# Neighbourhood attention on one core: two score groups per PSUM bank, and transposes that fill their banks one after another

## The chip, the cores and the metric

The kernel runs on one core of a Trainium2 chip. A core has a matrix engine (PE, with its weight loads shown apart as PEld), a vector engine (DVE), a scalar engine (ACT), a general engine (POOL) and queues that issue DMA transfers (SP is the one used most). PE writes its results to PSUM, a memory of eight banks; one bank holds 512 float32 values on each of 128 partitions. The metric is the device time of one execution in microseconds (us).

## The reference

One layer of a bidirectional encoder with 2048 tokens on a grid of 32 rows by 64 columns, 1024 features, 16 heads of 64. All numbers are float32.

```
h = rmsnorm(x, norm_0)
q, k, v, gate = split(h @ w_in, 4)
for each grid row r:                      # a query sees 8 key rows and 16 key columns
    s = q[r] . k[rows rs..rs+8, 32 columns round the block] / 8
    s = where(column is valid, s + bias, -1e30)
    p = softmax(s);  o[r] = p . v
x = x + (o * silu(gate)) @ w_out
return rmsnorm(x, norm_f)
```

## The kernel before

The kernel has three parts in time. First come the projections (`h @ w_in`), made of 128x512 products in two-part float32r (tile `pp`). Then comes a stretch of about 340 us in which attention and the last projections, later the first output products (`po`), alternate on PE. Last come the remaining output products (`py`).

Attention goes by pairs of heads `p` and blocks `T` of eight grid rows of queries. A block sees a stretch of key rows (`KEY_ROWS`): 11 rows for T=0, 15 for T=1 and T=2, 12 for T=3. Queries are cut into eight column strips `g` of 8x8 = 64 queries; two strips make a group `C` (`GROUPS`), and a group sees 2 or 3 strips of keys (`WIDE`). With R = 8 x key rows, a group's scores are 128 partitions (two strips of 64 queries) by `R * WIDE[C]` columns, for each of the two heads `s`. `order` lists the 32 pairs (p, T): eight with T=0, then sixteen with T=1 and 2, then eight with T=3.

The main loop makes one cycle for each entry `m` of `order`, and a last one. On PE a cycle is, in program order:

- some 12 to 21 matmuls of `pp` or `po`, given out by `feed`;
- `turns(m - 1)`: 44 transposes of the probabilities of the entry before, two at a time (h = 0 on partitions 0 to 63, h = 1 on 64 to 127), into six banks `ph[b, h]` with 8, 8 and 6 tiles of 64 columns for b = 0, 1, 2. A finished bank is copied to the tile `pta`: by ACT for h = 0, by DVE for h = 1 (`copy`);
- `scores(2m)` for the groups C = 0, 1 and `scores(2m + 1)` for C = 2, 3: for each group and each of two heads a bank, and 4 matmuls, each of 64 rows by 64 columns of the array. A float32 matmul runs as two passes, so the trace shows 32 records for 16 instructions. The query strip `h` picks the half of the output partitions, the head `s` the half of the rows that are read;
- `values(m - 1)`: 16 matmuls of `pta` with the values, into one bank `o`.

For each group and head DVE then adds the bias and takes the row's extreme (L1297, the reader of the score bank), and ACT takes the exponential (L1303). `normalise` multiplies by the reciprocal of the sum: for `scores(2m)` on POOL, for `scores(2m + 1)` on POOL (its first group) and on DVE (its second group). That happens in the next cycle at the latest, ahead of that cycle's transposes.

All PSUM tiles come from one pool of eight banks. A tile gets a bank as banks come free, and the first matmul into it waits until the last reader of the bank's tile before it is done. One bank is usually held by the `pp` or `po` product that is under way across the cycle. Instructions stand on each engine in the order in which the program makes them; there is no other scheduler.

Lines of the profile: L1288 score matmuls, L1343 transposes, L1334 and L1332 the copies by ACT and DVE, L1362 value matmuls, L1297 and L1303 the work on the scores, L1315 and L1313 `normalise` on POOL and DVE.

Of the kernel before, what the change touches and what calls it, by code (L numbers as in the profile page):

```python
# [39 lines left out]
WIDE = [2, 3, 3, 3]  # L40
# [25 lines left out]
def linear():  # L66
    at, n = {}, 0
    for strips in [(0,), (1, 2), (3, 4), (5, 6), (7,)]:
        for s in range(2):
            for strip in strips:  # L70
                for g in range(max(strip - 1, 0), min(strip + 2, 8)):
                    at[s, strip, g] = n
                    n += 1
    return at
# [3 lines left out]
def build(ctx, tc, x, xr, xt, wg, bias, w_out, n0, nf, out):  # L78
    nc = tc.nc
# [48 lines left out]
    def bank(n, name):  # L128
        return banks.tile([128, n], F32, name=name, tag="bank")
# [140 lines left out]
    for n, (k, j, ph, c) in enumerate(halves):  # L270
        a = (KINDS[k] + j, ph)
# [948 lines left out]
    order = [(p, 0) for p in range(NP)] + [(p, T) for p in range(NP) for T in (1, 2)] + [(p, 3) for p in range(NP)]  # L1220
# [52 lines left out]

    X, PT, ST = {}, {}, {}

    def scores(i, between=None):
        p, T, cs = pairs[i]
        kt, qt = KT[p, T], QT[p, T]
        r0, r1 = KEY_ROWS[T]
        got = []  # L1280
        R = (r1 - r0) * 8
        for C in cs:
            pst = [bank(R * WIDE[C], f"s{s}") for s in range(2)]
            for h, g in enumerate(GROUPS[C]):
                c0 = 8 * FIRST[g]
                for s in range(2):
                    a = slice(s * 64, s * 64 + 64)
                    nc.tensor.matmul(pst[s][h * 64:h * 64 + 64], qt[a, g * 64:g * 64 + 64],  # L1288
                                     kt[a, :r1 - r0, c0:c0 + 8 * WIDE[C]].rearrange("p r (s c) -> p s r c", c=8),
                                     start=True, stop=True)  # L1290
            got.append((C, pst))
        ST[i] = st = tiny.tile([128, 12], F32, name="st")
        for j, (C, pst) in enumerate(got):
            X[i, C] = [xp([128, 512], F32, f"x{s}")[:, :R * WIDE[C]] for s in range(2)]
            for s in range(2):
                o = 2 * j + s
                nc.vector.tensor_tensor_reduce(X[i, C][s], pst[s], EM[p, ROW_TYPE[T]][C > 0][s], -1.0, 1e38,  # L1297
                                               OP.add, OP.min, st[:, o:o + 1])
            if between and j == 0:
                between()  # L1300
            for s in range(2):
                o = 2 * j + s
                nc.scalar.activation(X[i, C][s], X[i, C][s], AF.Exp, bias=st[:, o:o + 1], scale=-1.0,  # L1303
                                     accum_out=st[:, 4 + o:5 + o])
# [14 lines left out]
    spots = linear()  # L1319

    def turns(m):
        p, T = order[m]
        k = 8 * (KEY_ROWS[T][1] - KEY_ROWS[T][0])
        PT[m] = pt([128, 3072], F32, "pta")
        t = PT[m].rearrange("p (n h c) -> p h n c", h=2, c=64)
        ph = {(b, h): bank((512, 512, 384)[b], f"ph{h}") for b in range(3) for h in range(2)}
        left = {(b, h): (8, 8, 6)[b] for b in range(3) for h in range(2)}

        def copy(b, h):
            o, i_ = t[:k, h, b * 8:b * 8 + (8, 8, 6)[b]], ph[b, h][:k].rearrange("p (n c) -> p n c", c=64)  # L1330
            if h:
                nc.vector.tensor_copy(o, i_)  # L1332
            else:
                nc.scalar.activation(o, i_, AF.Copy)  # L1334

        group = {g: C for C in range(4) for g in GROUPS[C]}
        lists = [sorted((group[g] // 2, n, s, strip, g) for (s, strip, g), n in spots.items() if n % 2 == h) for h in range(2)]
        for two in zip(*lists):
            for h, (late_, n, s, strip, g) in enumerate(two):
                q = slice(64 * h, 64 * h + 64)  # L1340
                b, o = n // 16, n // 2 % 8 * 64
                at = (strip - FIRST[g]) * k
                nc.tensor.transpose(ph[b, h][:k, o:o + 64], X[2 * m + late_, group[g]][s][q, at:at + k], ident[q, q])  # L1343
                left[b, h] -= 1
            for b, h in sorted(left):
                if left[b, h] == 0:
                    left[b, h] = -1
                    copy(b, h)
# [172 lines left out]
    def split_rows():  # L1521
        n = ready["split"]
        if rows_due():
            split_og(n)
            ready["split"] += 1
            return True
# [264 lines left out]
    for m in range(cycles + 1):  # L1791
        a = amount[m] - 8
        begin(m)
        feed(8)
        if m:
# [10 lines left out]
            for k in range(3):  # L1806
                if m == 1 and k == 2:
                    pass
                elif a > 12 or not any(due_here) and (k < 1 or k < 2 and m > 8 and m % 2 == 0):
                    got = split_rows()  # L1810
# [11 lines left out]
        if m:  # L1822
            turns(m - 1)
        if m == cycles:
            all_loads()
            feed(6)
            while next(outs, 0) != 0:
                due(1)
            land_T2()
            for n in range(3):  # L1830
                form_rows(n, 1)
        else:
            scores(2 * m)
            if m == 0:
                feed(first)
            scores(2 * m + 1, lambda: normalise(2 * m))
            if m == 0:
                consume(2, turn=True)
# [42 lines left out]
```

## Time and profile before

| | us |
|---|---|
| median of 3 runs | 1006.15 (1005.45 to 1006.79) |
| the profiled execution | 1005.34 |
| its span | 1003.4 |
| PE busy | 995.4 (99%) |
| PEld busy | 797.1 (79%) |
| DVE busy | 771.9 (77%) |
| ACT busy | 520.4 (52%) |
| POOL busy | 149.5 (15%) |
| granted clock of PE, mean | 0.998 |

A row of the timeline gives the start, the duration, the engine, the line, the operation, the tiles written and read, shapes, and how many instructions were merged into it; behind it in brackets stands the idle time of the engine before it and what ended it. A PE matmul's duration runs to its modelled end, and matmuls overlap, so that a busy PE can still hold back the next matmul: there the idle time of PEld, whose load stands just ahead of the matmul, tells of the wait.

### The profile page before, as it was taken

To read this page: it belongs to the slowest core of one execution; us is meant where nothing else is said; L and a number is where in the kernel's file an instruction comes from. 1 tells how busy PE (TensorE), PEld (TensorE's weight loads), DVE (VectorE), ACT (ScalarE), POOL (GpSimd) and SP (SyncE) were. 2 spreads that over 40 slices of the span, in tenths; PEclk is the share of its full clock that TensorE was granted. 3 is DMA by queue.
4 is the path that set the end of the run, shared out by engine and by line. 5 is a ranking of instruction groups with operands and counts; after the bars stand their busy time and mean duration, and the time that the engine had idled before them with its cause. 6 is when DMAs were issued, how large, how long until landed. Compare 5 with 4: busy or idle time off the path is not lost.

```text
span 1003.4 us, 19549 instructions
## 1 busy us (share of the span) xinstructions
PE 995.4 (99%) x6904; PEld 797.1 (79%) x6904; DVE 771.9 (77%) x1704; ACT 520.4 (52%) x1271; POOL 149.5 (15%) x233
## 2 busy tenths in 40 slices
PE   9999999999999999999999999999999999999997
PEld 7888888888888888888888777777777777778886
DVE  6899888997666866676765776778888888887876
ACT  7862344565434523343433465676767657564443
POOL 0000001321100000000000133243332323222010
PEclk9999999999999999999999999999999999999999
DMA  8943547777957755655566787879888688799564
GB/s 300 328 136 89 196 144 250 242 249 265 349 154 224 242 154 172 213 186 183 205 199 201 211 272 233 273 228 291 267 262 273 184 263 275 212 362 355 140 177 115
DMA packets 149833, 227.66 MB, mean 227 GB/s; under 512 B 13608, under 2 KB 65064, under 8 KB 149736
## 3 DMA queue, kind: packets, MB, share of 16 engines
q1 hardware_dynamic: 147144, 222.09, 68.8%
q0 software_dynamic: 2160, 3.93, 2.3%
q8 instruction: 54, 0.88, 0.4%
q10 hardware_dynamic: 432, 0.40, 0.1%
q14 instruction: 43, 0.35, 0.1%
HBM read 160.31 MB, written 66.06 MB: 226 GB/s over the span
## 4 chain that ended last, share of the span: by engine, by line
PE 99%; ACT 1%; DVE 0%; issue 0%
PE pp L448 40%; PE pv L614 13%; PE py L1658 10%; PE o L1362 8%; PE s L1288 7%; PE ph L1343 4%; PE pp L394 2%; PE po L1566 2%; PE pv L729 2%; PE po L1568 2%; PE pp L396 2%; PE pp L392 2%; PE po L1570 2%; ACT x L1303 0%; PE zp L135 0%; PE prb L242 0%
## 5 line engine op out<-in xcount | busy, mean ns | idle before, releaser
L448 PE MATMUL pp<-h,f 128*128 128x512 f32 x576 | 185.4, 389 | 0.0
L1315 POOL TENSOR_SCALAR x<-x,st 128x360 f32<-128x360 f32 (+5 forms) x192 | 106.3, 570 | 528.9 <-DVE st L1308 528.2
L448 PE MATMUL pp<-t,f 128*128 128x512 f32 x702 | 171.3, 389 | 0.0
L448 PEld LDWEIGHTS pp<-t,f 128*128 128x128 f32 x702 | 131.8, 188 | 27.4
L1303 ACT ACTIVATE x<-x,st 128x360 f32<-128x360 f32 (+5 forms) x256 | 134.2, 525 | 26.4 <-DVE st L1297 26.4
L448 PEld LDWEIGHTS pp<-h,f 128*128 128x128 f32 x576 | 108.1, 188 | 22.6
L448 PE MATMUL pp<-l,f 128*128 128x512 f32 x288 | 112.1, 389 | 0.0
L1297 DVE CUSTOM_DVE_ANT_0 x<-s,em 128x360 f32<-128x360 f32 (+5 forms) x256 | 102.5, 454 | 1.8 <-PE s L1288 1.4
L431 DVE TENSOR_TENSOR f<-raw,f 128x512 fp32r<-128x512 f32 x105 | 75.7, 726 | 19.6 <-ACT f L430 19.5
L1362 PEld LDWEIGHTS o<-pta,vt 120*64 120x64 f32 (+2 forms) x1024 | 68.8, 137 | 22.6 <-DVE st L1297 15.2
L1362 PE MATMUL o<-pta,vt 120*64 120x192 f32 (+5 forms) x1024 | 83.4, 316 | 0.3 <-issue 0.3
L430 ACT ACTIVATE f<-raw 128x512 fp32r<-128x512 f32 x105 | 63.5, 622 | 37.5 <-DVE raw L437 22.0
L1332 DVE COPY pta<-ph 120x512 f32<-120x512 f32 (+5 forms) x96 | 56.0, 638 | 33.5 <-PE ph L1343 33.2
L1334 ACT ACTIVATE pta<-ph 120x512 f32<-120x512 f32 (+5 forms) x96 | 46.8, 558 | 62.9 <-PE ph L1343 62.8
L1288 PE MATMUL s<-kt,q 64*64 64x360 f32 (+5 forms) x1024 | 78.6, 420 | 0.2 <-ACT pta L1334 0.2
L448 PEld LDWEIGHTS pp<-l,f 128*128 128x128 f32 x288 | 54.1, 188 | 11.2
L1288 PEld LDWEIGHTS s<-kt,q 64*64 64x64 f32 x1024 | 41.5, 131 | 22.0 <-ACT pta L1334 6.4
L614 PE MATMUL pv<-wh,t 128*128 128x512 f32 x176 | 56.1, 389 | 0.0
L448 PE MATMUL pp<-sixths,f 128*128 128x512 f32 x198 | 52.7, 389 | 0.0
L469 POOL TENSOR_TENSOR tmp<-tmp,rb 128x512 f32<-128x512 f32 x18 | 28.4, 1579 | 158.3 <-DVE tmp L466 140.9
L1343 PEld LDWEIGHTS ph<-ident,x 64*120 64x120 f32 (+2 forms) x1408 | 42.5, 128 | 11.3 <-issue 9.2
L1658 PE MATMUL py<-woh,f 128*128 128x512 f32 x160 | 50.6, 390 | 0.0
(226 smaller groups left out, 1870.6 us busy)
## 6 DMA issues: line engine op xcount, KB each, us to landing
raw<-in_wg_dram SPq DMA_DIRECT2D x124, 256.0 KB, 5.1
row<-in_xr_dram SPq DMA_DIRECT2D x32, 256.0 KB, 5.7
vd<-v SPq DMA_DIRECT2D x32, 256.0 KB, 3.4
sgd<-sg SPq DMA_DIRECT2D x32, 256.0 KB, 5.7
q<-qd SPq DMA_DIRECT2D x32, 256.0 KB, 5.6
sgt<-sgd SPq DMA_DIRECT2D x32, 256.0 KB, 6.6
ogd<-og SPq DMA_DIRECT2D x32, 256.0 KB, 2.9
kt<-kd SPq DMA_DIRECT2D x16, 480.0 KB, 6.8
```

What stands on the lines that cost most here:

```text
L430: nc.scalar.activation(t[:, 0], src, AF.Copy)
L431: nc.vector.tensor_tensor(t[:, 1], src, t[:, 0].bitcast(F32), OP.subtract)
L448: nc.tensor.matmul(B[n, P], t[:, int(m == 2), c], x[k][int(m == 1)], start=P in (1, 6, 5) and k == 0 and m == 0, stop=k == 3 and m == 2, s ...
L614: nc.tensor.matmul(p, a[:, o], b, start=P in (1, 6, 5) and k == 0 and m == 0, stop=k == 3 and m == 2, skip_group_check=True)
L1288: nc.tensor.matmul(pst[s][h * 64:h * 64 + 64], qt[a, g * 64:g * 64 + 64], kt[a, :r1 - r0, c0:c0 + 8 * WIDE[C]].rearrange("p r (s c) -> p s ...
L1297: nc.vector.tensor_tensor_reduce(X[i, C][s], pst[s], EM[p, ROW_TYPE[T]][C > 0][s], -1.0, 1e38, OP.add, OP.min, st[:, o:o + 1])
L1303: nc.scalar.activation(X[i, C][s], X[i, C][s], AF.Exp, bias=st[:, o:o + 1], scale=-1.0, accum_out=st[:, 4 + o:5 + o])
L1315: nc.gpsimd.tensor_scalar(X[i, C][s], X[i, C][s], st[:, o:o + 1], 1.0, op0=OP.mult, op1=OP.mult)
L1332: nc.vector.tensor_copy(o, i_)
L1343: nc.tensor.transpose(ph[b, h][:k, o:o + 64], X[2 * m + late_, group[g]][s][q, at:at + k], ident[q, q])
L1362: nc.tensor.matmul(o[s * 64:s * 64 + 64, g0 * 64:g1 * 64], vt[:k, strip, s * 64:s * 64 + 64], t[:k, n * 64:(n + g1 - g0) * 64], start=stri ...
L1658: nc.tensor.matmul(B[m, P], t[:, a, c], b, start=P in (1, 6, 5) and k == 0 and i == 0, stop=k == 3 and i == 2, skip_group_check=True)
```

## The change

Two things are changed, both on PE.

The scores. Where five strips of keys fit a bank (5R <= 512, that is 11 or 12 key rows: T=0 and T=3) the groups C = 0 (2R columns) and C = 1 (3R columns) of one head share one bank, so that `scores(2m)` takes two banks in place of four. In all entries the four matmuls of a group come in another order: both query strips of head 0, then both of head 1. Before, the heads alternated.

The transposes. The six banks hold 6, 8 and 8 tiles for b = 0, 1, 2, and the list is sorted by bank first, so that a bank is filled before the next is begun. Before, the list was sorted by group first: all tiles of C = 0, 1 came ahead of those of C = 2, 3, whatever their bank.

```diff
+    def score_places(cs, R):
+        at = {"order": [(C, s) for C in cs for s in range(2)]}
+        if cs[0] == 0 and 5 * R <= 512:
+            for s in range(2):
+                b = bank(5 * R, f"s{s}")
+                at[0, s], at[1, s] = b[:, :2 * R], b[:, 2 * R:]
+        else:
+            for C, s in at["order"]:
+                at[C, s] = bank(R * WIDE[C], f"s{s}")
+        return at
     def scores(i, between=None):
...
-        for C in cs:
-            pst = [bank(R * WIDE[C], f"s{s}") for s in range(2)]
+        places = score_places(cs, R)
+        for C, s in places["order"]:
             for h, g in enumerate(GROUPS[C]):
                 c0 = 8 * FIRST[g]
-                for s in range(2):
-                    a = slice(s * 64, s * 64 + 64)
-                    nc.tensor.matmul(pst[s][h * 64:h * 64 + 64], qt[a, g * 64:g * 64 + 64],
...
+                a = slice(s * 64, s * 64 + 64)
+                nc.tensor.matmul(places[C, s][h * 64:h * 64 + 64], qt[a, g * 64:g * 64 + 64],
...
     def turns(m):
-        ph = {(b, h): bank((512, 512, 384)[b], f"ph{h}") for b in range(3) for h in range(2)}
-        left = {(b, h): (8, 8, 6)[b] for b in range(3) for h in range(2)}
+        ends = (6, 14, 22)
+        size = (6, 8, 8)
+        ph = {(b, h): bank(size[b] * 64, f"ph{h}") for b in range(3) for h in range(2)}
+        left = {(b, h): size[b] for b in range(3) for h in range(2)}
...
-        lists = [sorted((group[g] // 2, n, s, strip, g) for (s, strip, g), n in spots.items() if n % 2 == h) for h in range(2)]
+        home = lambda n: sum(n // 2 >= e for e in ends)
+        lists = [sorted((home(n), group[g] // 2, n, s, strip, g) for (s, strip, g), n in spots.items() if n % 2 == h) for h in range(2)]
...
-                b, o = n // 16, n // 2 % 8 * 64
+                o = (n // 2 - ends[b] + size[b]) * 64
```

No engine gets more or fewer instructions by this. Two places show what moves, both on PE in a cycle that does the transposes and values of an entry with T=0 and the scores of the next one; rows of equal tiles that follow each other are merged with a count behind.

The scores of the groups C = 0 (176 columns) and C = 1 (264 columns), before: `s0` is the bank of head 0, `s1` that of head 1.

```order
L1288 MATMUL s0_5785<-kt_5545,q_5528 64x176
L1288 MATMUL s1_5786<-kt_5545,q_5528 64x176
L1288 MATMUL s0_5785<-kt_5545,q_5528 64x176
L1288 MATMUL s1_5786<-kt_5545,q_5528 64x176
L1288 MATMUL s0_5791<-kt_5545,q_5528 64x264
L1288 MATMUL s1_5792<-kt_5545,q_5528 64x264
L1288 MATMUL s0_5791<-kt_5545,q_5528 64x264
L1288 MATMUL s1_5792<-kt_5545,q_5528 64x264
```

The same place, and the first of C = 2 behind it, now:

```order
L1297 MATMUL s0_5779<-kt_5541,q_5524 64x176 x2
L1297 MATMUL s1_5780<-kt_5541,q_5524 64x176 x2
L1297 MATMUL s0_5779<-kt_5541,q_5524 64x264 x2
L1297 MATMUL s1_5780<-kt_5541,q_5524 64x264 x2
L1297 MATMUL s0_5802<-kt_5541,q_5524 64x264 x2
L1297 MATMUL s1_5803<-kt_5541,q_5524 64x264 x2
```

Four bank tiles (5785, 5786, 5791, 5792) have become two (5779, 5780), and the two matmuls on the same half of the rows now stand next to each other.

The transposes, before, from the last tile of the first ACT bank (`ph0_5729`) to the last of the first DVE bank (`ph1_5730`); the tiles `x0_5651` and `x1_5652` belong to C = 2:

```order
L1343 MATMUL ph0_5729<-ident_163,x1_5633 88x64
L1343 MATMUL ph1_5734<-ident_163,x1_5627 88x64
L1343 MATMUL ph0_5731<-ident_163,x0_5632 88x64
L1343 MATMUL ph1_5734<-ident_163,x0_5626 88x64
L1343 MATMUL ph0_5731<-ident_163,x1_5633 88x64
L1343 MATMUL ph1_5734<-ident_163,x1_5627 88x64
L1343 MATMUL ph0_5731<-ident_163,x0_5651 88x64
L1343 MATMUL ph1_5730<-ident_163,x0_5651 88x64
L1343 MATMUL ph0_5731<-ident_163,x0_5651 88x64
L1343 MATMUL ph1_5730<-ident_163,x1_5652 88x64
```

Now, the last tiles of the first two banks (`ph0_5723`, `ph1_5724`) and what follows; `x0_5645` belongs to C = 2:

```order
L1355 MATMUL ph1_5724<-ident_163,x0_5626 88x64
L1355 MATMUL ph0_5723<-ident_163,x0_5626 88x64
L1355 MATMUL ph1_5724<-ident_163,x1_5627 88x64
L1355 MATMUL ph0_5723<-ident_163,x1_5621 88x64
L1355 MATMUL ph1_5724<-ident_163,x0_5645 88x64
L1355 MATMUL ph0_5725<-ident_163,x1_5627 88x64
L1355 MATMUL ph1_5726<-ident_163,x1_5627 88x64
```

Of the 22 pairs of transposes the first ACT bank was full with the 8th and the first DVE bank with the 12th; now both are full with the 6th. The first transpose that needs a tile of C = 2 was in the 11th pair; now it is in the 6th.

More of the change, by code (lines that the diff above doesn't have):

```diff
@@ L1279, in scores @@
         r0, r1 = KEY_ROWS[T]
-        got = []
         R = (r1 - r0) * 8
-        for C in cs:
-            pst = [bank(R * WIDE[C], f"s{s}") for s in range(2)]
+        places = score_places(cs, R)
+        for C, s in places["order"]:
             for h, g in enumerate(GROUPS[C]):
                 c0 = 8 * FIRST[g]
-                for s in range(2):
-                    a = slice(s * 64, s * 64 + 64)
[L1288 to L1291, printed above, removed]
+                a = slice(s * 64, s * 64 + 64)
+                nc.tensor.matmul(places[C, s][h * 64:h * 64 + 64], qt[a, g * 64:g * 64 + 64],
+                                 kt[a, :r1 - r0, c0:c0 + 8 * WIDE[C]].rearrange("p r (s c) -> p s r c", c=8),
+                                 start=True, stop=True, skip_group_check=True)
+        got = [(C, [places[C, s] for s in range(2)]) for C in cs]
         ST[i] = st = tiny.tile([128, 12], F32, name="st")
@@ L1325, in turns @@
         t = PT[m].rearrange("p (n h c) -> p h n c", h=2, c=64)
-        ph = {(b, h): bank((512, 512, 384)[b], f"ph{h}") for b in range(3) for h in range(2)}
-        left = {(b, h): (8, 8, 6)[b] for b in range(3) for h in range(2)}
+        ends = (6, 14, 22)
+        size = (6, 8, 8)
+        ph = {(b, h): bank(size[b] * 64, f"ph{h}") for b in range(3) for h in range(2)}
+        left = {(b, h): size[b] for b in range(3) for h in range(2)}
         def copy(b, h):
-            o, i_ = t[:k, h, b * 8:b * 8 + (8, 8, 6)[b]], ph[b, h][:k].rearrange("p (n c) -> p n c", c=64)
+            o, i_ = t[:k, h, ends[b] - size[b]:ends[b]], ph[b, h][:k].rearrange("p (n c) -> p n c", c=64)
             if h:
@@ L1336, in turns @@
         group = {g: C for C in range(4) for g in GROUPS[C]}
-        lists = [sorted((group[g] // 2, n, s, strip, g) for (s, strip, g), n in spots.items() if n % 2 == h) for h in range(2)]
+        home = lambda n: sum(n // 2 >= e for e in ends)
+        lists = [sorted((home(n), group[g] // 2, n, s, strip, g) for (s, strip, g), n in spots.items() if n % 2 == h) for h in range(2)]
         for two in zip(*lists):
-            for h, (late_, n, s, strip, g) in enumerate(two):
+            for h, (b, late_, n, s, strip, g) in enumerate(two):
                 q = slice(64 * h, 64 * h + 64)
-                b, o = n // 16, n // 2 % 8 * 64
+                o = (n // 2 - ends[b] + size[b]) * 64
                 at = (strip - FIRST[g]) * k
```

## The prediction

> **What bounds the kernel now.** I read the page first: its busy times and the chain that ended last.
>
> ```profile
> span 1003.4 us, 19549 instructions
> ...
> PE 995.4 (99%) x6904; PEld 797.1 (79%) x6904; DVE 771.9 (77%) x1704; ACT 520.4 (52%) x1271; POOL 149.5 (15%) x233
> ...
> PE 99%; ACT 1%; DVE 0%; issue 0%
> ```
>
> PE is on the chain for 99% of the span, so whatever shortens PE's stream shortens the kernel, and what other engines gain or lose counts only where PE waits. A busy PE hides short waits, however, since the modelled end of a matmul reaches over the next one. So I next read the groups by line for the weight loads alone, over the attention cycles (575.45 to 897.5 us): the idle time ahead of a load tells of a matmul that was held back.
>
> ```profile
> L1343 PEld LDWEIGHTS ph<-ident,x 64*120 64x120 f32 (+2 forms) x1364 | 41.2, 128 | 10.9 <-issue 8.8 <-POOL x L1315 2.1
> L1288 PEld LDWEIGHTS s<-kt,q 64*64 64x64 f32 x992 | 40.5, 131 | 21.1 <-ACT pta L1334 6.4 <-DVE pta L1332 3.7 <-issue 2.5
> ```
>
> The score loads wait for the two copies of the transposes (`pta`): the banks that the scores want are still being emptied. The timeline of one cycle (transposes of an entry with 11 key rows, scores of the next) shows how that comes about.
>
> ```profile
> 593.22 1.59 POOL L1315 TENSOR_SCALAR x<-x,st 128x264 f32<-128x264 f32 x2 [0.27 <-DVE st L1308]
> ...
> 595.69 1.43 PE L1343 MATMUL ph<-ident,x 64*88 64x64 f32 x44
> ...
> 596.43 1.46 ACT L1334 ACTIVATE pta<-ph 88x512 f32<-88x512 f32 x3 [3.07 <-PE ph L1343]
> 596.63 1.75 DVE L1332 COPY pta<-ph 88x512 f32<-88x512 f32 x3 [2.08 <-PE ph L1343]
> ...
> 597.05 2.31 PE L1288 MATMUL s<-kt,q 64*64 64x176 f32 x32
> 597.94 0.27 PEld L1288 LDWEIGHTS s<-kt,q 64*64 64x64 f32 x8 [0.18 <-ACT pta L1334]
> 598.30 0.33 DVE L1297 CUSTOM_DVE_ANT_0 x<-s,em 128x176 f32<-128x176 f32 x1
> ...
> 598.43 0.46 PEld L1288 LDWEIGHTS s<-kt,q 64*64 64x64 f32 x8 [0.23 <-DVE pta L1332]
> ...
> 599.29 2.37 PEld L1362 LDWEIGHTS o<-pta,vt 88*64 88x64 f32 x32 [0.40 <-DVE st L1297]
> 599.29 2.61 PE L1362 MATMUL o<-pta,vt 88*64 88x128 f32 x32
> ```
>
> From the first score matmul to the first value matmul pass 2.24 us (597.05 to 599.29). In that time the copies by ACT run until 597.89 and those by DVE until 598.38, and one bank is wanted twice: with one bank held by the projection, seven are left for eight score tiles, so the last one (C = 3, head 1) gets the bank of C = 0, head 0, and waits until DVE has read it. DVE does that only behind its copies, from 598.30 to 598.63; PE goes on at about 598.7.
>
> How long the same work takes without a wait is seen in the first cycle, where nothing has been transposed yet and the two halves of the scores stand alone: 176 + 264 columns in one piece, 264 + 264 in the other.
>
> ```profile
> 561.94 0.97 PE L1288 MATMUL s<-kt,q 64*64 64x176 f32 x16
> ...
> 566.70 1.12 PE L1288 MATMUL s<-kt,q 64*64 64x264 f32 x16
> ...
> 561.94 0.51 PEld L1288 LDWEIGHTS s<-kt,q 64*64 64x64 f32 x16 [0.35 <-issue]
> ```
>
> 88 columns more cost 0.15 us, which is 1.70 ns for each column of a group. The four groups of a cycle have 968 columns with 11 key rows, 1320 with 15, 1056 with 12. Beyond the 440 columns of the first piece that makes 0.97 + 528 x 1.70 ns = 1.87 us, 0.97 + 880 x 1.70 ns = 2.47 us and 0.97 + 616 x 1.70 ns = 2.02 us for a cycle without waits. The view by stretches, for L1288 alone, gives what the cycles take: seven cycles with scores of 11 key rows, sixteen with 15, eight with 12.
>
> ```profile
> 575.45:646.60 71.15, 16.17 (x224) 8.85 (x224) 1.00 0.85 255
> 646.60:814.00 167.40, 40.67 (x512) 21.16 (x512) 1.00 0.82 253
> 814.00:897.50 83.50, 19.66 (x256) 10.45 (x256) 1.00 0.85 274
> ```
>
> So the waits inside the scores are 16.17 - 7 x 1.87 = 3.1 us, 40.67 - 16 x 2.47 = 1.2 us and 19.66 - 8 x 2.02 = 3.5 us, together 7.8 us: 0.44 us in each short cycle and 0.07 us in a long one, where the longer matmuls give the copies time. That is the most that earlier banks can bring in the scores.
>
> **The change part by part.** *Shared banks (short cycles).* The scores then want six banks and seven are to be had. No tile waits for a bank that this cycle's scores have used, so the wait for DVE's read goes. The six are, as the program gives them out, a free one, then those of the transposes, in the order in which they are copied. C = 2 starts 0.75 us after the first score matmul (440 columns at 1.70 ns) and C = 3 at 1.20 us, which is 597.80 and 598.25 in the cycle above. Even with the copies as late as now, C = 2 would find the first DVE copy and the second ACT copy about done, and C = 3 the third ACT copy (597.89).
>
> *The transposes' order.* The two first banks are full with the 6th of 22 pairs in place of the 8th (ACT) and 12th (DVE). A pair takes about 1.43 / 22 = 0.065 us at most, so the first ACT copy starts at least 0.1 us earlier, the first DVE copy about 0.2 to 0.3 us (never before ACT's). The widths change places:
>
> ```profile
> L1334 ACT ACTIVATE pta<-ph 88x512 f32<-88x512 f32 x14 | 7.5, 588 | 14.8 <-PE ph L1343 14.8
> L1334 ACT ACTIVATE pta<-ph 88x384 f32<-88x384 f32 x7 | 3.4, 487 | 0.0
> L1332 DVE COPY pta<-ph 88x512 f32<-88x512 f32 x14 | 9.0, 682 | 13.8 <-PE ph L1343 13.8
> L1332 DVE COPY pta<-ph 88x384 f32<-88x384 f32 x7 | 3.8, 544 | 0.0
> ```
>
> The short copy is now the first of three, so ACT's first copy ends 0.2 us earlier (0.1 from its start, 0.1 from its width) and DVE's first about 0.4 us. The three together take as long as before; DVE's last ends about 0.3 us earlier. ACT's last can only start when the last transposes are done, so it ends hardly earlier. In the long cycles, which still take eight banks, C = 1 wants the first DVE and second ACT copies, C = 2 the second DVE and third ACT copies, and C = 3 DVE's third copy and its read of C = 0. With everything on DVE 0.3 us earlier these come in time: most of the 1.2 us goes.
>
> *Two waits that a late copy keeps.* In one short and one long cycle ACT comes late to its first copy, because it does other work.
>
> ```profile
> 815.43 0.54 PE L1288 MATMUL s<-kt,q 64*64 64x192 f32 x2
> 816.16 2.17 PE L1288 MATMUL s<-kt,q 64*64 64x192 f32 x30 [0.19 <-ACT pta L1334]
> ...
> 815.53 1.45 ACT L1334 ACTIVATE pta<-ph 120x512 f32<-120x512 f32 x3
> ...
> 689.88 1.47 ACT L1334 ACTIVATE pta<-ph 120x512 f32<-120x512 f32 x3 [1.25 <-PE ph L1343]
> ```
>
> The chain of work in order of time (start, us, what) shows the scores of the second:
>
> ```profile
> 688.90 1.44 PE ph L1343 x37
> 690.34 2.72 PE s L1288 x30
> ```
>
> In the first, the scores take 0.54 + 2.17 = 2.71 us in place of 2.02, and only 0.1 us comes back through the narrower first copy: 0.6 us stays. In the second, the first copy starts at 689.88 and will end 0.49 us later, at 690.37, when the scores have just begun; their head 1 waits for it, and the copies behind it are as late: an estimated 0.15 us stays.
>
> *The other order of the four matmuls of a group.* The four use the four quarters of the array, and in the piece at 561.94 all run side by side: 16 loads of 131 ns (the mean of the PEld row above), 2.1 us of loads, lie within 0.51 us. Any order of the four should do the same. The new order puts two that read the same 64 rows next to each other; the value matmuls, which all read the same 88 rows, show that neighbour: 32 loads of at least 0.13 us lie within 2.37 us of PEld, under 2.61 us of matmuls. I cost this at nothing; if the cover failed, it would cost as the rival below says.
>
> The Trainium skill, "TensorE: Matmul & The Clock Gate", Part 3 (packing small matmuls), says that a weight load overlaps matmuls in flight only when it goes to another group of rows. By that rule the new order would lose, and the rows just quoted speak against it.
>
> *The wait that is added.* DVE's first read of a shared bank waits for C = 1 as well, which is done 0.97 us after the scores start (the first piece): at 598.02 in the cycle above, against 598.30 at which DVE gets there now and about 598.05 once its copies end earlier. Behind it on DVE stand the other seven reads, and behind those ACT's exponentials; PE waits for them only at the next transposes. So it costs nothing, and would cost PE nothing if DVE began at 598.30 as today.
>
> *The transposes want C = 2 earlier*, in the 6th pair in place of the 11th, 0.3 us. In the cycle above POOL has normalised by 594.81, 0.88 us before the transposes. The tightest cycles are like this one:
>
> ```profile
> 665.75 1.83 POOL L1315 TENSOR_SCALAR x<-x,st 128x360 f32<-128x360 f32 x2 [1.42 <-DVE st L1308]
> ...
> 667.36 1.51 PE L1343 MATMUL ph<-ident,x 64*120 64x64 f32 x44
> ```
>
> POOL ends at 667.58, 0.22 us after the first transpose; of its two tiles the second, from head 1, is now first used in the 8th pair, 7 x 0.065 = 0.45 us in. 0.2 us is left, and DVE, which feeds POOL, gets earlier too. Short cycles get about 0.4 us shorter while DVE's reads get 0.2 us earlier, so they lose 0.2 us of 0.88. Nothing.
>
> **Sum.** 7.8 - 0.6 - 0.15 = 7.0 us. After the scores come the values; they want DVE's third copy (at most 598.38 + 0.14 us for its width, if it started no earlier) and would start at 597.05 + 1.80 = 598.85, so the wait does not pass on to them. The profiled execution took 1005.34 us, 0.81 us below the median of the runs; 1005.34 - 7.0 = 998.3, and against the median 1006.15 - 7.0 = 999.1 us, which I forecast.
>
> **The rivals.** *Only the shared banks bring something* (0.15): the long cycles keep their 1.2 us, as the third ACT copy and DVE's read come no earlier in effect. Then 5.8 us are gained, 1000.3 us. For it: ACT's last copy ends as now. Against it: the rows give DVE 0.3 us.
>
> *The new neighbours get in each other's way* (0.08, slower). If a load can't run beside a matmul on the same rows, as soon as it stands right behind it, each pass of a group exposes one load: 8 passes in 32 cycles are 256 x 0.131 = 33.5 us, and 33.5 - 7.0 = 26.5 us are lost: 1032.6 us. It decides from 7.0 / 256 = 27 ns for each pass. Against it stand the loads of the values, and that the third load of a group at 561.94 already had a running matmul on its rows.
>
> *The banks don't come free as the change wants* (0.05): the next cycle's products or the values take up the bank that is saved, and PE waits at another place for about the same time. Then the time stays within 0.2%, 1005 us by an estimate. Against it: behind the scores only one tile, `o`, is wanted before the copies are all done.
>
> My forecast has 0.72. The range goes from 997.2 (all 7.8 us and 1.1 us for the scatter of runs and small waits of the transposes) to 1002.5 (half of the sum): it takes in the first rival and leaves out the others. A change of 0.2%, about 2 us, is what can be told from none. So: faster 0.87 (the forecast and the first rival), within 0.2% 0.05 (the third), slower 0.08 (the second).
>
> **What would show it.** In the profile after: the scores' busy time per stretch near 13.2, 39.7 and 16.8 us; next to no idle time of score loads put down to DVE's or ACT's copies; DVE's first copy starting with ACT's; the value and transposes rows as long as now; the score loads as closely packed as at 561.94. Wrong would be: longer spacing of the passes within a group, idle time ahead of the transposes put down to POOL, or the waits found again at the values.

## The result and the profile after

The changed kernel took 998.74 us in the median of six runs (996.9 to 1003.56), the kernel before 1006.0 us beside it (1005.45 to 1009.27, six runs): a ratio of 0.993, 95% interval 0.9906 to 0.9954. Forecast were 999.1 us and 997.2 to 1002.5.

The execution that was profiled is the longest of the six: 1003.56 us, span 1001.5. What the change does in attention shows in it as well as in any other; what it loses behind attention is met in the kernel before as well, as will be seen. First its page, the same lines as before:

```profile
span 1001.5 us, 19560 instructions
...
PE 991.0 (99%) x6904; PEld 793.1 (79%) x6904; DVE 772.4 (77%) x1704; ACT 520.4 (52%) x1271; POOL 149.5 (15%) x233
...
PE 93%; DMA 4%; DVE 2%; ACT 1%; issue 0%; SPq 0%; DVEq 0%
```

DMA has 4% of the chain that ended last, where it had none: a transfer now comes late somewhere. In the scores (now L1297) the waits for copies are gone. The groups by line, weight loads over the attention cycles:

```profile
L1355 PEld LDWEIGHTS ph<-ident,x 64*120 64x120 f32 (+2 forms) x1365 | 41.3, 128 | 11.3 <-issue 9.2 <-POOL x L1324 2.1
L1297 PEld LDWEIGHTS s<-kt,q 64*64 64x64 f32 x992 | 36.3, 132 | 17.8 <-ACT pta L1345 0.4
```

ACT's 6.4 us have become 0.4, DVE's 3.7 are gone, and the transposes wait for POOL as long as before (2.1). The view by stretches, for the scores alone (length of the stretch, then PE busy):

```profile
576.32:644.37 68.05, 13.05 (x224) 7.82 (x224) 1.00 0.90 265
644.37:810.02 165.65, 39.32 (x512) 18.75 (x512) 1.00 0.83 256
810.02:890.71 80.69, 16.82 (x256) 9.70 (x256) 1.00 0.88 280
```

Forecast were 13.2, 39.7 and 16.8. The three sum up to 69.2 us against 76.5, 7.3 us less, and the stretches to 314.4 us against 322.05, 7.7 us less. The timeline of the cycle that the prediction showed, POOL and DMA left out:

```profile
595.67 1.43 PE L1355 MATMUL ph<-ident,x 64*88 64x64 f32 x44
596.27 1.75 DVE L1343 COPY pta<-ph 88x384 f32<-88x384 f32 x3 [1.43 <-PE ph L1355]
596.30 1.46 ACT L1345 ACTIVATE pta<-ph 88x384 f32<-88x384 f32 x3 [2.64 <-PE ph L1355]
...
597.03 1.86 PE L1297 MATMUL s<-kt,q 64*64 64x176 f32 x32
...
598.13 0.34 DVE L1306 CUSTOM_DVE_ANT_0 x<-s,em 128x176 f32<-128x176 f32 x1
...
598.82 1.23 PEld L1374 LDWEIGHTS o<-pta,vt 88*64 88x64 f32 x18 [0.40 <-DVE st L1306]
```

From the first score matmul to the first value matmul pass 1.79 us (597.03 to 598.82), where it was 2.24; the prediction's 1.80 was the cycle without a wait. DVE's copies begin with ACT's.

The last values stand behind transposes with no scores in between, and start 1.36 us after the first transpose in place of 1.74 (897.50 to 899.24 before):

```profile
890.71 1.43 PE L1355 MATMUL ph<-ident,x 64*96 64x64 f32 x44
892.07 2.69 PE L1374 MATMUL o<-pta,vt 96*64 96x128 f32 x32
```

So from the first transpose of attention to the last values it is 315.75 us now (576.32 to 892.07) and was 323.79 (575.45 to 899.24): 8.0 us gained, 1.0 more than forecast. Of these the profiled execution gives 5.3 back behind attention. The timeline of DVE and PE there:

```profile
919.50 0.69 DVE L1682 TENSOR_TENSOR u<-py,xp 128x512 f32<-128x512 f32 x1 [1.43 <-PE py L1670]
931.12 0.69 DVE L1643 TENSOR_TENSOR s<-raw 128x512 f32<-128x512 f32 x1 [10.93 <-DMA raw<-ogd]
...
933.16 0.47 PE L1670 MATMUL py<-woh,f 128*128 128x512 f32 x1 [2.82 <-DVE y L1450]
```

DVE stands at a sum (S1 of the third pair of row tiles, L1643) until the load `raw<-ogd` has landed; behind it in DVE's order stands the `y` that would free a bank for PE, and PE is idle for 2.82 us. Before, PE did not notice the wait for the same load:

```profile
930.96 0.69 DVE L1631 TENSOR_TENSOR s<-raw 128x512 f32<-128x512 f32 x1 [3.68 <-DMA raw<-ogd]
```

The load lands at nearly the same time in both profiles (930.96 and 931.12), but DVE comes to it 7 us earlier now. It is not that the transfers keep their time when attention gets shorter: in the profile of e4 (below), whose attention is as short, the load has landed by 922.65.

```profile
922.65 0.69 DVE L1643 TENSOR_TENSOR s<-raw 128x512 f32<-128x512 f32 x1 [2.00 <-DMA raw<-ogd]
```

The question that the experiments had to settle besides the parts of the change: is this wait its price?

### The profile page after: what moved, and what is told of

Its sections match the earlier page's. It is cut to its first block, busy times and chain, and to the rows that moved or that the text cites. A ratio compares the mean times of both kernels' runs of the same rounds, so it can differ in the third digit from the quotient of the medians.

```text
span 1001.5 us, 19560 instructions
## 1 busy us (share of the span) xinstructions
PE 991.0 (99%) x6904; PEld 793.1 (79%) x6904; DVE 772.4 (77%) x1704; ACT 520.4 (52%) x1271; POOL 149.5 (15%) x233
## 4 chain that ended last, share of the span: by engine, by line
PE 93%; DMA 4%; DVE 2%; ACT 1%; issue 0%; SPq 0%; DVEq 0%
PE pp L448 40%; PE pv L614 13%; PE o L1374 8%; PE s L1297 7%; PE py L1670 5%; PE ph L1355 4%; PE pp L394 2%; PE po L1578 2%; PE po L1580 2%; PE pp L396 2%; PE po L1582 2%; PE pp L392 2%; PE pv L729 2%; DMA raw<-ogd 1%; DMA ogd<-og 1%; DMA wol<-wodT 1%
## 5 line engine op out<-in xcount | busy, mean ns | idle before, releaser
L1297 PE MATMUL s<-kt,q 64*64 64x360 f32 (+5 forms) x1024 | 71.3, 412 | 0.0
L1297 PEld LDWEIGHTS s<-kt,q 64*64 64x64 f32 x1024 | 37.3, 132 | 18.6 <-ACT pta L1345 0.4
```

The costliest lines, as they stand in the source:

```text
L1297: nc.tensor.matmul(places[C, s][h * 64:h * 64 + 64], qt[a, g * 64:g * 64 + 64], kt[a, :r1 - r0, c0:c0 + 8 * WIDE[C]].rearrange("p r (s c) ...
```

## The experiments

All are measured beside the kernel before, whose median is 1005.8 us in the first set (23 runs), 1005.7 in the second and 1006.1 in the third (17 each).

**The shared banks alone** (e1): `turns` of the kernel before, and in the changed scores the old order of the four matmuls.

```diff
-        for C, s in places["order"]:
-            for h, g in enumerate(GROUPS[C]):
+        for C in cs:
+            for h, s, g in [(h, s, g) for h, g in enumerate(GROUPS[C]) for s in range(2)]:
```

> Shared banks alone: C = 0 and C = 1 of a head share a bank where five strips fit, the four matmuls of a group come in the order of before, and the transposes are those of before. My theory (the scores wait for banks, and either a smaller need or earlier copies takes the wait away): the short cycles, which then need six banks, lose all of their wait but the first 0.03 us for ACT's first copy, so the scores' busy time falls to about 13.3 us in the seven cycles with 11 key rows and to about 16.9 us in the eight with 12, and stays at 40.7 us in the sixteen with 15; 5.5 to 6 us are gained, about 1000.3 us. The rival that the shared banks bring next to nothing and the copies' order all of it expects 1005 us and 16.2 / 40.7 / 19.7 us.

Measured: 1000.6 us (999.92 to 1002.19), ratio 0.9944 (0.9926 to 0.9961). The scores by stretch:

```profile
577.37:645.75 68.38, 13.18 (x224) 8.48 (x224) 1.00 0.88 262
645.75:813.14 167.39, 40.68 (x512) 21.14 (x512) 1.00 0.82 253
813.14:894.30 81.16, 17.28 (x256) 10.45 (x256) 1.00 0.89 280
```

The short cycles gain nearly all that they have to give (16.17 to 13.18, 19.66 to 17.28), the long ones nothing: 40.68 as before (40.67). In the last stretch 16.9 us were expected; it missed them because ACT comes late to its copies in one cycle (at 843.56), where 2.50 us pass from the first score matmul to the values in place of 1.96. Attention is 5.1 us shorter (316.93), and so is the time.

**The transposes alone** (e2): the scores as in the kernel before.

> The transposes alone: bank by bank with 6, 8 and 8 tiles, scores as before with eight banks. My theory: DVE's copies end 0.3 us earlier, so the last score tile, which waits for DVE's read of the first, comes about 0.2 us earlier in a short cycle (half of its 0.44 us), and the long cycles lose nearly all of their wait: scores' busy time about 14.7, 39.6 and 17.7 us (with the late copy of one cycle left in), 3.5 to 4 us gained, about 1002.3 us. With the shared banks alone that is more than the whole, because either one takes away part of the same wait in the short cycles. The rival that the shared banks bring it all expects 1006 us.

Measured: 1001.03 us (999.03 to 1006.47), ratio 0.9947 (0.9931 to 0.9963). By stretch:

```profile
575.14:643.86 68.72, 13.83 (x224) 8.64 (x224) 1.00 0.88 262
643.86:809.47 165.61, 39.32 (x512) 18.85 (x512) 1.00 0.84 256
809.47:890.89 81.42, 17.83 (x256) 9.25 (x256) 1.00 0.86 276
```

The long cycles get all that the whole change gives them (39.32). But the short cycles, too, get most of theirs without a bank being shared, and attention is 6.3 us shorter (315.75). More than expected; the timeline of a short cycle of this kernel shows why:

```profile
594.68 1.43 PE L1346 MATMUL ph<-ident,x 64*88 64x64 f32 x44
...
596.04 1.97 PE L1288 MATMUL s<-kt,q 64*64 64x176 f32 x32
596.95 0.33 DVE L1297 CUSTOM_DVE_ANT_0 x<-s,em 128x176 f32<-128x176 f32 x1
...
597.94 1.07 PEld L1365 LDWEIGHTS o<-pta,vt 88*64 88x64 f32 x16 [0.40 <-DVE st L1297]
```

DVE reads the first score bank 2.27 us after the first transpose, where it did so after 2.61 (595.69 to 598.30). The last score tile still waits for that read, but the read has come 0.34 us earlier with DVE's copies, and 1.90 us pass to the values in place of 2.24. So the two halves of the change take away the same wait in the short cycles, each in its own way: 5.1 and 6.3 us alone, 7.7 together. The time gains less than attention in e2, 4.8 us in the medians: its profile takes 100.3 us from the last values to PE's end, 2.3 more than the kernel before.

**The order of the four matmuls alone** (e3): with the old transposes,

```diff
-        if cs[0] == 0 and 5 * R <= 512:
+        if False:
```

> The order of a group's four matmuls alone (both query strips of head 0, then of head 1), a bank for each head and group and the transposes as before. My theory: the four quarters of the array run side by side in any order, so nothing but a few hundredths of a us where a wait stands at another matmul: 1006 us within 1 us, score busy times within 0.5 us of before in each stretch. The rival that neighbours on the same rows hold each other up: 27 ns and more for each of 256 passes, 1013 us or more, up to 1039 us.

Measured: 1005.5 us (1004.97 to 1011.53), ratio 1.0001 (0.9986 to 1.0016).

**The whole change, but the old order of the four** (e4): the edit of e1 without its transposes.

> The whole change but the order of a group's four matmuls, which is that of before (heads alternate). My theory: as the whole change, 998.5 us within 1.5 us, with the same scores' busy times (13.1, 39.6, 16.6 us within 0.3). If neighbours on the same rows cost something that the whole change pays, this one is faster than the changed kernel by more than 2 us.

Measured: 997.5 us (997.21 to 998.75), ratio 0.9913 (0.9893 to 0.9932); attention 314.43 us, as in the changed kernel (314.39). Together with e3 this settles the neighbours: their order does nothing. The Trainium skill ("TensorE: Matmul & The Clock Gate", Part 3) lets a weight load overlap matmuls in flight only from another group of rows; these two runs speak against that reading for this pattern.

**Widths 8, 8, 6, but filled in order** (e8): `ends = (8, 16, 22)`, `size = (8, 8, 6)`.

> The changed kernel, but the six banks of the transposes hold 8, 8 and 6 tiles as before, still filled in their order. So the first two banks are full with the 8th pair (6th in the change; 8th and 12th before). Theory: the order is what brings, the widths hardly: ACT's copies start at 0.74 us after the first transpose as before, DVE's at 0.75 in place of 0.94 (0.61 in the change); short cycles stay at 1.80 and 1.94 us from the first score matmul to the values, long ones come to 2.38 to 2.42; 0 to 1 us more than the changed kernel: median 998 to 999. Rival: the narrow first copy is needed (C = 1 of a long cycle wants the first DVE copy, C = 3 DVE's read of C = 0): long cycles at 2.45 us as before, 16 x 0.07 = 1.1 us, and the short ones lose 0.1 us each, 1.5 us: together 2.6 us, median 1000.5.

Measured: 1000.26 us (999.01 to 1004.23), ratio 0.9944 (0.9925 to 0.9962). By stretch:

```profile
576.22:644.28 68.06, 13.15 (x224) 8.34 (x224) 1.00 0.88 265
644.28:811.20 166.92, 40.42 (x512) 22.90 (x512) 1.00 0.83 254
811.20:892.11 80.91, 17.22 (x256) 10.33 (x256) 1.00 0.86 276
```

The rival was right for the long cycles: 40.42, nearly as before. It was wrong for those with 11 key rows, which lose 0.1 us together (13.15 against 13.05), not 0.1 us each. The starts of single matmuls in one long cycle (us from its first score matmul at 668.80, 666.47 and 666.39; two heads, two passes for each group) tell where:

```
                 C=1, pass 1      C=1, pass 2      C=3, pass 2
                 first   last     first   last     first   last
before           0.456   0.492    0.758   0.845    1.968   2.055
widths 8, 8, 6   0.456   0.481    0.758   0.834    1.968   2.043
the change       0.455   0.475    0.758   0.778    1.968   1.988
```

Head 1 of the *second* group starts late, by 0.006 us in e8 and 0.017 us in the kernel before; it runs 0.06 to 0.07 us behind from the next pass on, and never catches up. By its time the copy that frees this bank is ACT's second. It ends 1.86 us after the first transpose in the kernel before and in e8, which is 0.42 after the scores begin; with the narrow first copy it ends at 1.67. The first two copies by ACT in this cycle, in e8 (first transpose at 665.03) and in the changed kernel (664.95):

```profile
665.80 1.08 ACT L1345 ACTIVATE pta<-ph 120x512 f32<-120x512 f32 x2 [2.58 <-PE ph L1355]
```

```profile
665.61 1.01 ACT L1345 ACTIVATE pta<-ph 120x384 f32<-120x384 f32 x2 [2.50 <-PE ph L1355]
```

DVE's copies end some 0.24 us earlier in e8 than before, and that brought the long cycles next to nothing.

**The load behind attention.** e3 already answered the question whether the wait is the change's price: its attention is as long as before (321.77 us), yet the execution that was profiled took 1010.54 us, and lost as much behind attention as the changed kernel:

```profile
938.14 0.69 DVE L1640 TENSOR_TENSOR s<-raw 128x512 f32<-128x512 f32 x1 [10.86 <-DMA raw<-ogd]
...
940.18 0.77 PE L1667 MATMUL py<-woh,f 128*128 128x512 f32 x1 [2.75 <-DVE y L1447]
```

From the last values to PE's end are 98.0 us before, 98.0 in e1, 98.1 in e4, 103.1 in e3, 103.3 in the changed kernel's profile. Four more kernels followed.

*The changed kernel again* (e5):

> The changed kernel itself, once more, beside the kernel before. Theory: attention from its first to its last transposes takes 314.4 us in every run (322.05 before), and what scatters is the stretch behind it: 98.1 us from the last values to PE's end where the load raw<-ogd that DVE waits for at the sum of the third pair lands early enough, 101 to 103.3 us where it doesn't. So most runs at 997 to 999 us, one in five at 1001 to 1004; median 998 +- 1. Rival: the late load belongs to the change (PE gets there 7 us earlier, the transfers don't), then most runs are above 1000 and the median is 1001 to 1003.

Measured: 997.6 us (997.12 to 1003.95), ratio 0.9928 (0.9905 to 0.9951). With the first six that makes twelve runs: eight from 996.9 to 998.9, four from 1001.8 to 1004.0, median 998.1. The rival, most runs above 1000, is out; long runs are one in three so far, where one in five was expected.

*S1 two products earlier in DVE's order* (e7), `(8, "S1")` to `(6, "S1")`:

> The changed kernel with the sum S1 of the third pair two products earlier in DVE's order, nothing else moved. Theory: DVE then stands from about 914.7 us on until the load lands, at 922.6 in the better runs and 931 in the worse, and PE has some 8 us of slack behind it: the better runs lose 0 to 2 us, the worse 5 to 10 more than now. Median 998.5 to 1003, highest above 1006. Rival (DVE's wait at this sum isn't what stalls PE): as the changed kernel, 998 +- 1, highest 1004.

Measured: 1004.34 us (998.99 to 1007.88), ratio 0.9974 (0.9957 to 0.9991). The wait grows and PE's with it:

```profile
927.09 0.69 DVE L1643 TENSOR_TENSOR s<-raw 128x512 f32<-128x512 f32 x1 [13.20 <-DMA raw<-ogd]
...
929.13 5.83 PE L1670 MATMUL py<-t,f 128*128 128x512 f32 x13 [7.81 <-DVE u L1682]
```

The median lies 1.3 us above the range given: PE had 5.4 us of slack there (13.20 - 7.81), not the 8 that were assumed. So DVE's wait at this sum is what stalls PE.

*S1 two products later* (e6, and once more as e10):

```diff
-        for i, f in ((8, "S1"), (9, "S2"), (10, "S3"), (12, "S4")):
+        for i, f in ((10, "S1"), (10, "S2"), (11, "S3"), (12, "S4")):
             on(i, sum_rows, 2, f)
```

> The changed kernel with the sum S1 of the third pair (the instruction of DVE that waited 10.93 us for raw<-ogd) two products later in DVE's order, S2 right behind it and S3 one product later; nothing else moves. Theory: the load may then land 5.5 us later before PE has to wait; at the landing seen in the profile (11 us after DVE had come to it) PE no longer stalls. Runs above 1000 us go, the median is the same as the changed kernel's or 0.5 us lower: 997.0 to 998.0, highest below 1000. Rival: the loss behind attention comes from elsewhere (the clock that falls by itself, the matmuls' own weights t<-wodT landing late); then the scatter stays as it is, up to 1002 to 1004.

> The changed kernel with the later sum once more, for the number of its runs: so far 996.9 to 999.8 in six, while the changed kernel has four of twelve above 1001.5. Theory: no run above 1000.5, median 997 to 998. Rival (chance so far): a third of the runs above 1001.5.

Measured: 997.8 us (996.92 to 999.78), ratio 0.9918 (0.9902 to 0.9934), and 997.83 us (996.96 to 1000.81), ratio 0.992 (0.9906 to 0.9934). None of twelve runs is above 1001.5, where four of twelve were; one passes the 1000.5 that e10 was given, and its cause stays open.

*The kernel before with the later sum* (e9):

> The kernel before with the third pair's sum S1 two products later (S2 right behind it, S3 one later), attention untouched. Theory: the late landing of raw<-ogd is in the kernel before as well (6 of 46 of its runs lie above 1008.5), so its slow tail goes with the later sum: median 1005.2 to 1005.8, highest below 1008. Rival: the kernel before is slow in those runs for another reason; then runs above 1008.5 stay.

Measured: 1005.33 us (1004.63 to 1006.83, 12 runs), ratio 0.999 (0.9981 to 0.9998); the kernel before beside it has five of 17 runs above 1007.5. DVE no longer waits for the load:

```profile
932.77 0.68 DVE L1631 TENSOR_TENSOR s<-raw 128x512 f32<-128x512 f32 x1
```

So a late load occurs with either form of attention, and e3 lost as much to it with the old one. That the later place covers it is shown by the counts of runs alone: none of the profiled executions of e6, e9 and e10 was a long one. Why the load is late in some runs was not settled. Two things add up in the changed kernel's profile beside e4's: the first of the loads behind this sum is issued 3.2 us later (916.02 against 912.78), and from there to DVE's start pass 15.1 us in place of 9.9. The view by stretches of the kernel before and of e3 behind attention (last three columns: clock, share of the DMA engines, GB/s) shows transfers that keep the engines nearly as busy and bring less. Before:

```profile
900.00:910.00 10.00, 10.00 (x60) 8.43 (x57) 9.09 (x21) 4.62 (x10) 0.00 (x0) 1.00 1.04 390
910.00:920.00 10.00, 10.00 (x46) 8.29 (x45) 8.88 (x16) 6.17 (x13) 1.37 (x2) 1.00 1.05 390
```

And e3:

```profile
900.00:910.00 10.00, 10.00 (x60) 8.42 (x57) 9.07 (x21) 4.61 (x10) 0.00 (x0) 1.00 1.01 353
910.00:920.00 10.00, 10.00 (x46) 8.29 (x45) 8.90 (x15) 6.19 (x13) 1.39 (x2) 1.00 0.98 348
```

Nor is it settled whether the change makes it more frequent: four of the changed kernel's twelve runs lie more than 3 us above its median, and six of the 46 that the kernel before had up to then (seven lie above 1008.5, where the expectation of e9 has six). The changed kernel with the later sum is the one to keep: its median can't be told from the changed kernel's, its longest run is 3 us shorter.

## Why the prediction was right

The forecast was 0.4 us off, partly by luck: attention gained 1.0 us more, and a wait that the prediction had not looked for takes some of it back in a third of the runs. The upper end of the range, half of the sum, would be 1002.65 and not 1002.5; nothing hangs on it.

*The bound and its reading held.* The waits stood where the prediction read them, in the loads of the scores. A cycle with 11 key rows takes 1.79 us to the values (forecast 1.80).

*7.0 us in the scores: 7.3 by their busy time.* By stretch the forecast missed by 0.15, 0.4 and 0.0 us. The long cycles are off most: without the late one's 0.11 us they take 39.21 / 16 = 2.45 us, where 1.70 ns for each column had given 2.47.

*The late copies: right in size, not in place.* 0.75 us was to stay, from two cycles in which ACT comes late. Three remain: 0.11 us at 686, 0.34 at 810 and 0.40 at 840, together 0.85. The third is new; its ACT copy starts 1.26 us after the first transpose (840.09), 0.63 is usual, because ACT is at other work:

```profile
840.71 0.63 ACT L1453 ACTIVATE xr<-y 128x512 f32<-128x512 f32 x1 [2.17 <-DVE y L1450]
841.25 0.19 ACT L1453 ACTIVATION_READ_ACCUMULATOR xr<-y 128x1 f32 x1
841.34 1.43 ACT L1345 ACTIVATE pta<-ph 96x384 f32<-96x384 f32 x3
```

The kernel before had one more as well, at 751.25, which the prediction did not see: 2.59 us from the first score matmul to the values in place of 2.44. In the changed kernel that cycle takes 2.38 like the others.

*Who held up the long cycles: wrong.* The prediction had most of the 1.2 us go "with everything on DVE 0.3 us earlier". e8 has DVE's copies 0.24 us earlier and gets back 0.25 of the 1.35 us, 0.15 of it in the one cycle in which ACT came late before (751.25) and does not in e8; the rest needed the narrow first copy, which brings ACT's second 0.19 us forward. The prediction named that copy as wanted by C = 1, and didn't see that it was the late one.

*Which half brings what: the share was wrong.* The first rival put 5.8 us down to the shared banks, leaving 1.2 to the transposes. Alone the banks brought 5.1, and the transposes 6.3, since DVE's read of the first bank moves with its copies. The sum came right because the waits were counted once, not the halves.

*Left out: the last values*, which have no scores ahead of them. The wait for ACT's last copy there was 0.4 us and is gone (1.74 to 1.36 us).

*The added wait: there, and free.* DVE's first read waits for C = 1 by 0.19 us, not nothing: 2.46 us after the first transpose (595.67 to 598.13) against 2.27 in e2. PE's next transposes come on time all the same; they wait for POOL 2.1 us in all, as before.

*Left out: what stands behind attention.* The prediction took the last 98 us as shifting unchanged. Its trace held the warning, a DVE wait of 3.68 us for a load; it did not ask how much later that load could be before PE would feel it. 2.82 us of idle PE at a wait of 10.93 say some 8.1 us.

Of the rivals, the neighbours (0.08) and the banks that don't come free (0.05) are excluded by e3, e4 and the weight-load row; "only the shared banks" is excluded by e2.

## What to carry to other kernels

Two edits that relieve the same wait are not worth the sum of their gains: count the waits, then ask of each edit alone which of them it ends. When the last user of a resource is late by a hundredth of a microsecond, look for the reader that frees it, not at the engine with the most to do; making the first of a row of copies short moves all behind it. And when a stretch gets shorter, look behind it for an in-order engine that stands at a transfer, with work queued behind it that the bound engine needs: here a later place in the order cost nothing, and none of twelve runs was a long one.

## What the runs showed of the hardware

A short idle time of PE costs more than itself. After the 2.82 us the granted clock (the column ahead of the last two) of the changed kernel's trace was down to a half for some 3.4 us, 0.4 of them in the first row:

```profile
933.00:934.00 1.00, 0.84 (x3) 0.72 (x4) 1.00 (x3) 0.95 (x3) 0.00 (x0) 0.80 0.00 0
934.00:935.00 1.00, 1.00 (x3) 0.77 (x3) 1.00 (x3) 0.86 (x2) 0.00 (x0) 0.50 0.00 0
935.00:936.00 1.00, 1.00 (x4) 0.75 (x3) 1.00 (x3) 0.00 (x0) 0.00 (x0) 0.50 0.08 16
936.00:937.00 1.00, 1.00 (x4) 0.81 (x3) 1.00 (x3) 0.35 (x1) 0.00 (x0) 0.50 0.47 135
937.00:938.00 1.00, 1.00 (x5) 0.83 (x5) 1.00 (x3) 0.98 (x4) 0.00 (x0) 1.00 0.37 121
```

That makes about 1.7 us of matmuls lost on top. In e5 an idle time of 3.37 us was followed by some 6 us at half the clock. The Trainium skill ("TensorE: Matmul & The Clock Gate", Part 1) has the clock fall after an idle window of about 3.4 us; here 2.82 us (from the modelled end of the last matmul) were enough, and e3's 2.75. In e3 the clock had fallen some 0.6 us before PE's next matmul (940.18), after some 2.1 us of idle time:

```profile
939.00:940.00 1.00, 0.00 (x0) 0.00 (x0) 1.00 (x3) 0.00 (x0) 0.00 (x0) 0.79 0.00 0
```

A start that is 0.006 to 0.017 us late became a lag of 0.06 to 0.07 us in the stream of packed matmuls of the table above, and stayed until the stream ended.
